# A two-layer hybrid decoder trunk: layer 0's first norm made with tokens on the partitions, and the input loaded twice

## The chip, the core and the metric

The kernel runs on one core of one Trainium2 chip. The metric is device time in microseconds (us) of one launch. The core's engines are TensorE (PE, with its weight loads as PEld), VectorE (DVE), ScalarE (ACT), GpSimd (POOL) and SyncE (SP), which issues all the DMAs spoken of here. Each engine runs its instructions in a fixed order and waits for the others by semaphores.

## What is computed

A sequence of 1024 tokens of width 1024 gets 16 learned tokens in front of it and goes through two layers. Cut to what matters here, the reference is:

```python
def rmsnorm(x, w):
    y = x * lax.rsqrt(jnp.mean(x * x, axis=-1, keepdims=True) + EPS)
    return y * w

h = jnp.concatenate([meta_b, x], axis=1)
for layer in range(DEPTH):
    hn = rmsnorm(h, norm_mix_w[layer])
    proj = hn @ w_in[layer]
    hq, hf, hi, hg, gq, gk, gv, gz, ga, gb, su = jnp.split(proj, pts, axis=-1)
    y_a = hgrn2_mixer(hq, hf, hi, hg, ...)
    y_b = gdn_mixer(gq, gk, gv, gz, ga, gb, ...)
    y_c = s5_mixer(su, ...)
    h = h + jnp.concatenate([y_a, y_b, y_c], axis=-1) @ w_out[layer]
    hn = rmsnorm(h, norm_mlp_w[layer])
    h = h + jnp.square(jax.nn.relu(hn @ mlp_w1[layer])) @ mlp_w2[layer]
return rmsnorm(h, final_norm_w)[:, N_META:]
```

The change is about the very first `rmsnorm` (layer 0, before `w_in`), and about where the `h` of `h + ...` in layer 0 comes from. All is in float32.

## The kernel before

The 1040 tokens are two blocks of 520 tokens; a block is five windows of 104. The 1024 features are eight tiles of 128 partitions, so `h` of a block is eight tiles 128 x 520, with features on the partitions and tokens along the free dimension.

A float32 product is made of three passes on TensorE: each operand is split into a high part rounded to a shorter format and the low part that is left, and the kernel sums high x high, high x low and low x high. `columns` (line 488) does so for 128 output columns: 8 feature tiles x 3 passes x 2 runs of some 260 tokens, 48 matmuls into one PSUM tile `pd`, of which there are two buffers. A weight granule is loaded as `wr` and split into `wh` and `wl` (line 460 and a subtraction). The activation operands are `xh` and `xl` (eight tiles each, 520 tokens and 4 tokens of history in front). Tiles that other stages use under the names `mt`, `qt` and `D2` can serve as a second set of operands; the method that hands them out is `spare_operands`. Scratch tiles `s` have six buffers, and the loads of `x` land in them.

Layer 0 begins like this. `load_x` (line 1276) loads the windows of a block with tokens on the partitions (two DMAs of 104 x 512 a window, line 1288, one more where the 16 learned tokens stand), transposes them on TensorE (line 1291, eight transposes a window) and copies each piece from PSUM to `h`, in turn on ScalarE and VectorE (line 1294): 40 transposes and 40 copies a block. `normed_rows` (line 511) then makes the norm over the features: eight squares, seven additions, a product with a matrix of ones that sums over the partitions (lines 121 to 125), Ln and Exp, and for each of the eight tiles a multiplication by gain and scale (line 116, VectorE, 128 x 520), a cast to the high part (line 532, ScalarE) and a subtraction for the low part (line 113, VectorE). `projection` (line 730) makes all products with `w_in`: first `in_s5` (two output tiles, 96 matmuls, evicted at line 683), then the others, with the decay and solve parts of the DeltaNet between them. In layer 0, block 0, it takes a hook that loads block 1's `x` and saves it. `save_h` stores `h` to DRAM (eight DMAs of 260 KB a block), `states` (the recurrences) follows the projection, and then the same is done for block 1. `run` (line 1466) then reads block 0's `h` back with `get_h`, runs `out_mlp` on it (product with `w_out`, the MLP), makes the norm of layer 1 in the spare operands, saves `h`, and reads block 1's `h` back; that block's `out_mlp` is interleaved with layer 1's projection of block 0.

What stands when on an engine is not written out by hand. A scheduler orders the instructions of each engine at build time by priorities and by its own simulation of the time; on the chip each engine then keeps to that order. DMAs of SP go out in order, over a ring of eight semaphores, so that a DMA waits for the one eight before it.

Of the kernel before, what the change touches and what calls it, by code (L numbers as in the profile page):

```python
# [17 lines left out]
D = 1024  # L18
# [67 lines left out]
def trace(*gens):  # L86

    live = list(gens)
    while live:
        for g in list(live):  # L90
            if next(g, StopIteration) is StopIteration:
                live.remove(g)


class Kern:
# [392 lines left out]
    def columns(self, wts, xs, runs):  # L488

        xh, xl = xs  # L490
        ps = self.tl(self.pd, [128, 2, 512], "pd", 2)
        kn = len(xh)
        for k in range(kn):
            wh, wl = wts[k // 4]
            for i, (w, x) in enumerate(((wh, xh), (wh, xl), (wl, xh))):
                for c, cs in runs.items():
                    self.mm(ps[:, c, :cs.stop - cs.start], w[:, k % 4, :], x[k][:, cs],
                            start=(k == 0 and i == 0), stop=(k == kn - 1 and i == 2))
        return ps
# [10 lines left out]
    def normed_rows(self, h, wcol, b, spare=None):  # L510
# [10 lines left out]
        for k in range(KD):  # L521
# [13 lines left out]
            xs[1].append(lo)  # L535
        return xs

    def normed(self, h, wcol):
# [182 lines left out]

    def block(self, l, b, h, hook=None, first=False):

        xs = self.normed_rows(h, 8 * l, b)
        if first:
            self.save_h(b, h)
        trace(self.projection(l, b, xs, hook, first))
        self.states(l, b)

    def projection(self, l, b, xs, hook=None, first=False):  # L730
# [4 lines left out]
        if first:  # L735
            self.setup_mixers()
        g = {"z": self.tl(self.dr, [6, 128, T], "gated", 2)}
        us = self.in_s5(l, xs)
        yield 2 * DENSE
        g["rows"] = self.in_rows(l, b, xs)  # L740
# [534 lines left out]

    def load_x(self, b, h):
        nc = self.nc
        x = self.ins["x"][0]
        for w in range(NW):
            t0 = b * T + w * W - NMETA  # L1280
            for k0 in (0, 4):
                xt = self.s()[:W, :512]
                cs = slice(128 * k0, 128 * k0 + 512)
                if t0 < 0:
                    nc.sync.dma_start(xt[0:NMETA, :], self.ins["meta"][:, cs])
                    nc.sync.dma_start(xt[NMETA:W, :], x[0:W - NMETA, cs])
                else:
                    nc.sync.dma_start(xt, x[t0:t0 + W, cs])
# [6 lines left out]
            yield  # L1295

# [169 lines left out]
    def run(self):  # L1466
        self.setup()
        self.H, self.YS = {}, {}
        nxt = {}

        def early():

            nxt[1] = self.htiles()
            yield from self.load_x(1, nxt[1])
            self.save_h(1, nxt[1])
# [11 lines left out]

        h = self.get_h(1)
        rest = self.out_mlp(0, 1, h)
# [46 lines left out]
```

## Time and profile before

| | |
|---|---|
| Runs of the kernel | 2992.46 us median of 3 (2989.41 to 2992.55) |
| Profiled execution, own time | 2987.76 us |
| Its span in the trace | 2986.0 us |
| Mean granted TensorE clock | 0.966 of full speed |
| TensorE busy | 2815.6 us (94%) |
| VectorE busy | 1702.9 us (57%) |
| ScalarE busy | 1309.7 us (44%) |
| GpSimd busy | 820.5 us (27%) |

A share of the span is an average over many stages. What a change in one stage is worth is read from that stage. In the rows further down, a timeline row has the start, the duration, the engine, the line and operation with its output and inputs, and in brackets how long the engine sat idle before it and what ended that wait. A row of a stretch has each engine's busy time, then the granted TensorE clock as a share of full speed, then the share of the DMA engines and GB/s. PE durations are modelled and overlap; the distance between two starts is the better measure of a matmul.

### The profile page before, as it was taken

To read this page: it belongs to the slowest core of one execution; us is meant where nothing else is said; L and a number is where in the kernel's file an instruction comes from. 1 tells how busy PE (TensorE), PEld (TensorE's weight loads), DVE (VectorE), ACT (ScalarE), POOL (GpSimd) and SP (SyncE) were. 2 spreads that over 40 slices of the span, in tenths; PEclk is the share of its full clock that TensorE was granted. 3 is DMA by queue.
4 is the path that set the end of the run, shared out by engine and by line. 5 is a ranking of instruction groups with operands and counts; after the bars stand their busy time and mean duration, and the time that the engine had idled before them with its cause. 6 is when DMAs were issued, how large, how long until landed. Compare 5 with 4: busy or idle time off the path is not lost.

```text
span 2986.0 us, 60325 instructions
## 1 busy us (share of the span) xinstructions
PE 2815.6 (94%) x23513; PEld 2632.9 (88%) x23513; DVE 1702.9 (57%) x3497; ACT 1309.7 (44%) x2689; POOL 820.5 (27%) x801
## 2 busy tenths in 40 slices
PE   7797899979999989999999999999899999999998
PEld 6787799878999989998999988987688788999998
DVE  7788885776532245668755577658645323622224
ACT  4455475534443344543434446554344433533332
POOL 0000522154634430000020211101636444144441
PEclk8798999989999999999999999999999999999999
DMA  5666555644433344444633356564544333533332
GB/s 147 185 152 181 161 153 152 185 87 133 123 93 102 92 142 115 123 130 104 167 110 104 116 153 168 155 173 131 129 111 126 90 105 97 162 93 93 93 93 79
DMA packets 641610, 381.17 MB, mean 128 GB/s; under 512 B 166239, under 2 KB 599237, under 8 KB 641325
## 3 DMA queue, kind: packets, MB, share of 16 engines
q1 hardware_dynamic: 641325, 377.31, 45.9%
q8 instruction: 186, 3.05, 0.4%
q14 instruction: 99, 0.81, 0.1%
HBM read 308.52 MB, written 70.43 MB: 127 GB/s over the span
## 4 chain that ended last, share of the span: by engine, by line
PE 78%; DVE 10%; DMA 7%; issue 2%; ACT 1%; POOL 1%; SPq 0%; DVEq 0%; ACTq 0%; POOLq 0%
PE pd L125 66%; PE mxt L125 8%; DVE mh L113 3%; PE mxh L125 3%; DVE wl L113 1%; DVE s L116 1%; DVE s L113 1%; DMA nh<-rowd 1%; DMA XD<-diag 1%; DMA ys<-ydr 1%; DVE mt L113 1%; DMA mh<-qkvd 0%; DMA mh<-rowd 0%; DVE h L113 0%; POOL mh L113 0%
## 5 line engine op out<-in xcount | busy, mean ns | idle before, releaser
L460 ACT CAST wh<-wr 128x512 fp32r<-128x512 f32 x776 | 479.7, 619 | 955.3 <-PE pd L125 879.7
L125 PE MATMUL pd<-xh,wh 128*128 128x260 f32 (+3 forms) x3256 | 737.6, 299 | 25.9 <-DVE s L116 9.0
L125 PE MATMUL pd<-xl,wh 128*128 128x260 f32 (+3 forms) x3256 | 736.9, 299 | 3.7 <-DVE xl L113 2.3
L125 PE MATMUL pd<-xh,wl 128*128 128x260 f32 (+2 forms) x3208 | 719.4, 297 | 2.7 <-POOL wl L113 1.7
L113 POOL TENSOR_TENSOR wl<-wr,wh 128x512 fp32r<-128x512 f32 x376 | 494.2, 1315 | 720.6 <-ACT wh L460 663.1
L125 PEld LDWEIGHTS pd<-xh,wh 128*128 128x128 f32 x3256 | 520.9, 191 | 46.6 <-ACT xh L532 7.5
L125 PEld LDWEIGHTS pd<-xl,wh 128*128 128x128 f32 x3256 | 522.1, 191 | 19.9 <-DVE xl L113 3.0
L125 PEld LDWEIGHTS pd<-xh,wl 128*128 128x128 f32 x3208 | 514.6, 191 | 17.0 <-POOL wl L113 2.3
L125 PE MATMUL pd<-uh,wh 128*128 128x260 f32 (+1 forms) x2008 | 469.3, 303 | 14.1 <-DVE h L113 8.0
L125 PE MATMUL pd<-uh,wl 128*128 128x260 f32 (+1 forms) x2008 | 472.1, 303 | 0.0
L125 PE MATMUL pd<-ul,wh 128*128 128x260 f32 (+1 forms) x2008 | 468.0, 302 | 0.7 <-DVE ul L113 0.6
L113 DVE TENSOR_TENSOR h<-h,pd 128x520 f32<-128x520 f32 (+2 forms) x296 | 200.4, 678 | 347.6 <-PE pd L125 345.3
L125 PEld LDWEIGHTS pd<-uh,wh 128*128 128x128 f32 x2008 | 321.0, 189 | 30.1 <-issue 6.8
L113 DVE TENSOR_TENSOR wl<-wr,wh 128x512 fp32r<-128x512 f32 x400 | 282.0, 705 | 106.2 <-ACT wh L460 101.6
L125 PEld LDWEIGHTS pd<-uh,wl 128*128 128x128 f32 x2008 | 322.5, 189 | 14.2
L125 PEld LDWEIGHTS pd<-ul,wh 128*128 128x128 f32 x2008 | 321.1, 189 | 14.2 <-DVE ul L113 1.3
L110 ACT ACTIVATE s<-s 128x520 f32<-128x520 f32 (+3 forms) x431 | 272.6, 636 | 120.6 <-DVE s L121 55.1
L116 DVE SCALAR_TENSOR_TENSOR s<-pd,r 128x520 f32<-128x520 f32 (+2 forms) x121 | 83.6, 692 | 249.8 <-PE pd L125 249.7
L113 DVE TENSOR_TENSOR s<-s 128x520 f32<-128x520 f32 (+3 forms) x199 | 137.8, 696 | 54.9 <-ACT s L110 53.4
L113 DVE TENSOR_TENSOR ul<-s,uh 128x520 fp32r<-128x520 f32 (+1 forms) x129 | 93.8, 729 | 114.6 <-ACT uh L460 114.0
L113 POOL TENSOR_TENSOR nt<-nt 128x208 f32<-128x208 f32 x80 | 54.2, 678 | 367.1 <-ACT nt L110 247.7
L403 POOL MEMSET mh<- 128x512 f32 x2 | 1.1, 526 | 496.0 <-DVE RT L113 294.6
(272 smaller groups left out, 3549.8 us busy)
## 6 DMA issues: line engine op xcount, KB each, us to landing
wr<-in_mlp_w_dram SPq DMA_DIRECT2D x512, 256.0 KB
wr<-in_w_in_dram SPq DMA_DIRECT2D x208, 256.0 KB
wr<-in_w_out_dram SPq DMA_DIRECT2D x64, 256.0 KB
qkvd<-s SPq DMA_DIRECT2D x48, 260.0 KB
win<-qkvd SPq DMA_DIRECT2D x40, 312.0 KB
hdr<-h SPq DMA_DIRECT2D x32, 260.0 KB
mh<-qkvd SPq DMA_DIRECT2D x40, 208.0 KB
hd<-s SPq DMA_DIRECT2D x32, 260.0 KB
```

Source lines behind the costliest of these rows:

```text
L110: return self.nc.scalar.activation(out, in_, func, **kw)
L113: return (eng or self.nc.vector).tensor_tensor(out, a, b, op)
L116: return self.nc.vector.scalar_tensor_tensor(out, a, s, b, op0, op1)
L125: return self.nc.tensor.matmul(out, lhsT, rhs, start=start, stop=stop, **kw)
L403: nc.gpsimd.memset(z, 0.0)
L460: self.nc.scalar.copy(hi, src)
```

## The change

Layer 0's norm is no longer made from `h`. A new `load_normed` loads a window of `x` with tokens on the partitions, and there sums the squares of each token (two ScalarE Squares with an accumulator, one addition), takes Ln and Exp on 104 x 1, scales the window's two halves in place (two VectorE operations 104 x 512), and transposes the scaled rows into one `pd` tile. From there each of the eight pieces 128 x 104 goes straight into the operands: ScalarE writes the high part with the gain as its scale, VectorE the low part (gain times piece, less the high part). So a window has eight pairs of one ScalarE and one VectorE operation, a block 40. Block 0 uses the spare operands, block 1 `xh` and `xl`, in the hook within block 0's projection. The norm's other setup is moved ahead of the loads. In layer 0's first projection `in_s5` goes over the first run of tokens alone, and then over the second. The stores of `h` and the reloads before `out_mlp` go away for layer 0. In their place `load_x` loads `x` again before each block's `out_mlp`, with 40 transposes and 40 copies each.

```diff
-        for k in range(kn):
-            wh, wl = wts[k // 4]
-            for i, (w, x) in enumerate(((wh, xh), (wh, xl), (wl, xh))):
-                for c, cs in runs.items():
...
+        for part in [{c: cs} for c, cs in runs.items()] if self.early else [runs]:
+            for k in range(kn):
+                wh, wl = wts[k // 4]
+                for i, (w, x) in enumerate(((wh, xh), (wh, xl), (wl, xh))):
+                    for c, cs in part.items():
...
+    def load_normed(self, b, spare=None):
...
+        nxt = self.x_rows(b, 0)
+        yield
+        for w in range(NW):
+            rows, nxt = nxt, self.x_rows(b, w + 1) if w + 1 < NW else None
+            ss = self.tl(self.sp, [W, 4], "xss", 2)
+            for i, xt in enumerate(rows):
+                junk = self.s()[:W, :512]
+                self.act(junk, xt, AF.Square, accum_out=ss[:, i:i + 1])
+            self.tt(ss[:, 2:3], ss[:, 0:1], ss[:, 1:2], ALU.add)
+            self.act(ss[:, 2:3], ss[:, 2:3], AF.Ln, scale=1.0 / D, bias=EPS)
+            self.act(ss[:, 3:4], ss[:, 2:3], AF.Exp, scale=-0.5)
+            ps = self.tl(self.pd, [128, 2, 512], "pd", 2)
+            for g, xt in enumerate(rows):
+                self.ts(xt, xt, ss[:, 3:4], ALU.mult)
+                for i in range(4):
+                    nc.tensor.transpose(ps[:, g, i * W:(i + 1) * W], xt[:, i * 128:(i + 1) * 128], self.ident[:W, :W])
+            at = slice(HIST + w * W, HIST + (w + 1) * W)
+            for k in range(KD):
+                p, wc = ps[:, k // 4, (k % 4) * W:(k % 4 + 1) * W], self.prm[:, k:k + 1]
+                self.act(xs[0][k][:, at], p, AF.Copy, scale=wc)
+                self.stt(xs[1][k][:, at], p, wc, xs[0][k][:, at].bitcast(F32), ALU.mult, ALU.subtract)
+            yield
...
-        h = self.htiles()
-        trace(self.load_x(0, h))
+        self.first, self.early = None, False
+        load = self.load_normed(0, self.spare_operands())
+        next(load)
+        self.setup_norms()
+        trace(load)
         self.ready = {(0, col): self.in_weights(0, col) for col in (C_SU, C_SU + 128)}
-        self.setup_norms()
-        self.block(0, 0, h, early(), True)
-        self.block(0, 1, nxt[1])
-        h = self.get_h(0)
+        xs = self.first
+        trace(self.projection(0, 0, xs, self.load_normed(1), True))
+        xs = self.first
+        self.states(0, 0)
+        trace(self.projection(0, 1, xs))
+        self.states(0, 1)
+        h = self.load_x(0)
         trace(self.out_mlp(0, 0, h))
         self.low = None
         xs = self.normed_rows(h, 8, 0, self.spare_operands())
         self.save_h(0, h)
 
-        h = self.get_h(1)
+        h = self.load_x(1)
         rest = self.out_mlp(0, 1, h)
```

The order of instructions changes at three places that matter below.

TensorE at the start, before; `pd_202` is the last piece of the last window, `pd_275` the sum of squares, and `pd_478` and `pd_532` the two products of `in_s5`:

```order
L1291 MATMUL pd_191<-ident_88,s_189 128x104 x4
L220 MATMUL mxh_247<-ident_88,mh_237 128x128
L1291 MATMUL pd_202<-ident_88,s_200 128x104 x4
L230 MATMUL mxh_364<-ident_88,mh_362 128x96
L125 MATMUL pd_275<-s_251,ones_235 128x260 x2
L125 MATMUL pd_478<-xh_285,wh_214 128x264
L125 MATMUL pd_478<-xh_285,wh_214 128x256
L125 MATMUL pd_532<-xh_285,wh_226 128x264
```

and after the change; lines 566 and 331 are the window's transposes and those of the S5 parameters, `mt_91` is the first high part:

```order
L566 MATMUL pd_221<-ident_88,s_172 128x104 x4
L566 MATMUL pd_260<-ident_88,s_209 128x104 x4
L566 MATMUL pd_260<-ident_88,s_211 128x104 x4
L331 MATMUL mxh_464<-ident_88,mh_402 128x16
L331 MATMUL mxh_464<-ident_88,mh_403 128x16
L331 MATMUL mxh_464<-ident_88,mh_402 128x16
L566 MATMUL pd_295<-ident_88,s_248 128x104 x4
L566 MATMUL pd_295<-ident_88,s_250 128x104 x4
L331 MATMUL mxh_464<-ident_88,mh_403 128x16 x2
L125 MATMUL pd_479<-mt_91,wh_341 128x264
L125 MATMUL pd_479<-mt_92,wh_341 128x264
```

All five windows' transposes and those of the S5 parameters now stand ahead of the first product, and `pd_479` takes the buffer of `pd_260`, the fourth window's.

TensorE at the change from block 0 to block 1 of layer 0, after the change; `pd_3590` is the last product of block 0's projection and `xh_1876` block 1's first operand:

```order
L125 MATMUL pd_3590<-mt_99,wh_3587 128x260 x2
L125 MATMUL pd_3590<-mt_100,wh_3587 128x260 x2
...
L125 MATMUL pd_3590<-D2_106,wh_3587 128x260 x2
L125 MATMUL pd_3590<-D2_105,wl_3586 128x260 x2
L125 MATMUL pd_5067<-xh_1876,wh_5058 128x264
L125 MATMUL pd_5067<-xh_1876,wh_5058 128x256
```

Before, the sum of squares `pd_4983` and the norm's casts stood between the two; now the products follow each other.

TensorE at the second load of block 1 after the change; `pd_14062` is the last product of block 0's MLP, `pd_14112` the sum of squares of layer 1's norm, `pd_14330` layer 1's first product:

```order
L125 MATMUL pd_14062<-uh_13827,wl_14058 128x260 x2
L125 MATMUL pd_14112<-s_14088,ones_115 128x260 x2
L1338 MATMUL pd_14210<-ident_88,s_14206 128x104 x4
L1338 MATMUL pd_14219<-ident_88,s_14208 128x104 x4
...
L1338 MATMUL pd_14298<-ident_88,s_14294 128x104 x4
L1338 MATMUL pd_14307<-ident_88,s_14296 128x104 x4
L125 MATMUL pd_14330<-mt_14122,wh_14321 128x264
L125 MATMUL pd_14330<-mt_14122,wh_14321 128x256
```

Before, layer 1's first product stood right behind the sum of squares; now ten groups of four transposes stand between them, each group in a `pd` buffer of its own.

## Rows read from the trace of the kernel before

**Rows 1.** The page: engines over the span, and the chain that ended last.
```profile
PE 2815.6 (94%) x23513; PEld 2632.9 (88%) x23513; DVE 1702.9 (57%) x3497; ACT 1309.7 (44%) x2689; POOL 820.5 (27%) x801
...
PE 78%; DVE 10%; DMA 7%; issue 2%; ACT 1%; POOL 1%; SPq 0%; DVEq 0%; ACTq 0%; POOLq 0%
```

**Rows 2.** Stretches of the change of block and what follows (start:end, length, engines, PEclk).
```profile
248.80:273.90 25.10, 9.68 (x34) 7.44 (x35) 22.09 (x43) 13.91 (x30) 0.39 (x1) 0.59 0.36 112
...
300.00:330.00 30.00, 22.13 (x241) 20.14 (x241) 28.42 (x64) 12.77 (x26) 19.55 (x21) 0.77 0.47 129
```

**Rows 3.** Timeline of PE at the change of block in layer 0.
```profile
248.40 0.40 PE L125 MATMUL pd<-xh,wl 128*128 128x260 f32 x2
...
266.40 1.24 PE L125 MATMUL pd<-xh,wh 128*128 128x264 f32 x4 [2.50 <-ACT xh L532]
...
273.52 0.54 PE L125 MATMUL pd<-xh,wl 128*128 128x264 f32 x2
273.90 0.40 PE L125 MATMUL pd<-xh,wh 128*128 128x264 f32 x2
```

**Rows 4.** One tile's instructions (ns min/median/max), and a group of the page (busy, mean).
```profile
L116 DVE SCALAR_TENSOR_TENSOR s<-h,prm,r x16: 741/748/755, 30.7 to 275.1; 128x520 f32<-128x520 f32 x16
```
```profile
L113 DVE TENSOR_TENSOR s<-s 128x520 f32<-128x520 f32 (+3 forms) x199 | 137.8, 696 | 54.9 <-ACT s L110 53.4
```

**Rows 5.** Timeline of ACT and DVE at the first window.
```profile
7.72 0.24 ACT L1294 COPY h<-pd 128x104 f32<-128x104 f32 x1 [1.42 <-PE pd L1291]
8.00 0.27 DVE L1294 COPY h<-pd 128x104 f32<-128x104 f32 x1 [0.97 <-ACT h L1294]
8.30 0.24 ACT L1294 COPY h<-pd 128x104 f32<-128x104 f32 x1 [0.33 <-DVE h L1294]
```

**Rows 6.** Forms near the new ones, from four tiles' instructions (ns min/median/max).
```profile
L1294 ACT COPY h<-pd x40: 218/245/253, 7.7 to 142.3; 128x104 f32<-128x104 f32 x40
L1294 DVE COPY h<-pd x40: 247/266/268, 8.0 to 143.5; 128x104 f32<-128x104 f32 x40
L110 ACT ACTIVATE xh<-h,prm x8: 713/728/733, 574.8 to 617.7; 128x520 fp32r<-128x520 f32 x8
L532 ACT CAST xh<-s x8: 623/623/627, 31.6 to 40.7; 128x524 fp32r<-128x524 f32 x8
L116 DVE SCALAR_TENSOR_TENSOR nt<-mxt,gsc,mt x20: 334/343/352, 341.3 to 547.0; 104x128 f32<-104x128 f32 x20
```

**Rows 7.** Timeline of DVE and PE at the start.
```profile
19.10 0.22 DVE L222 COPY prm<-mxh 128x56 f32<-128x56 f32 x1 [0.51 <-PE mxh L220]
...
32.27 1.24 PE L125 MATMUL pd<-xh,wh 128*128 128x264 f32 x4 [3.86 <-ACT xh L532]
...
49.77 0.65 DVE L683 COPY s<-pd 128x264 f32<-128x264 f32 x1
```

**Rows 8.** Timeline of PE around the hook's load of block 1.
```profile
109.28 0.41 PE L125 MATMUL pd<-xh,wl 128*128 128x264 f32 x2
...
123.89 1.62 PE L1291 MATMUL pd<-ident,s 104*128 104x104 f32 x8 [8.88 <-DMA s<-in_x_dram]
...
142.84 0.51 PE L125 MATMUL pd<-xh,wh 128*128 128x264 f32 x2 [0.65 <-DVE h L1294]
```

**Rows 9.** PE around the first product of `out_mlp`, block 0, and that stretch's engines.
```profile
540.38 0.41 PE L125 MATMUL pd<-xh,wl 128*128 128x260 f32 x2
...
560.37 0.80 PE L125 MATMUL pd<-uh,wh 128*128 128x260 f32 x4 [0.18 <-ACT uh L460]
```
```profile
540.80:560.40 19.60, 14.47 (x84) 12.40 (x83) 9.71 (x25) 10.37 (x38) 5.90 (x7) 0.66 0.75 209
```

**Rows 10.** Timeline of PE and ACT at layer 1's first products.
```profile
1115.87 1.23 PE L125 MATMUL pd<-mt,wh 128*128 128x264 f32 x4 [5.01 <-ACT mt L532]
...
1119.08 0.80 PE L125 MATMUL pd<-mt,wh 128*128 128x264 f32 x2 [1.98 <-DVE mt L113]
...
1123.57 0.63 ACT L532 CAST D<-s 128x524 fp32r<-128x524 f32 x1
```

More of the change, by code (lines that the diff above doesn't have):

```diff
@@ L536, in normed_rows @@
         return xs
+    def load_normed(self, b, spare=None):
+        nc = self.nc
+        before, self.first = self.first, ([], [])
+        for k in range(KD):
+            for half_, tag in zip(self.first, ("xh", "xl")):
+                half_.append(next(spare) if spare else self.operand(tag))
+        xs = self.first
+        if before is None:
+            zero = self.sp.tile([128, HIST], F32, name="zero")
+            nc.vector.memset(zero, 0.0)
+        nxt = self.x_rows(b, 0)
[15 more added lines that the diff above has]
+            at = slice(HIST + w * W, HIST + (w + 1) * W)
+            for k in range(KD):
+                p, wc = ps[:, k // 4, (k % 4) * W:(k % 4 + 1) * W], self.prm[:, k:k + 1]
+                self.act(xs[0][k][:, at], p, AF.Copy, scale=wc)
+                self.stt(xs[1][k][:, at], p, wc, xs[0][k][:, at].bitcast(F32), ALU.mult, ALU.subtract)
+            yield
+        for i in range(2):
+            for k in range(KD):
+                nc.scalar.copy(xs[i][k][:, :HIST], before[i][k][:, T:].bitcast(F32) if before else zero)
     def normed(self, h, wcol):
@@ L720, in lead, with block @@
             yield
[L722 to L727, printed above, removed]
+    def block(self, l, b, h):
+        trace(self.projection(l, b, self.normed_rows(h, 8 * l, b)))
         self.states(l, b)
@@ L737, in projection @@
         g = {"z": self.tl(self.dr, [6, 128, T], "gated", 2)}
+        self.early = first
         us = self.in_s5(l, xs)
+        self.early = False
         yield 2 * DENSE
@@ L1274, in htiles, with x_rows, load_x @@
         return [self.tl(self.big, [128, T], "h", 8) for _ in range(KD)]
-    def load_x(self, b, h):
+    def x_rows(self, b, w):
         nc = self.nc
         x = self.ins["x"][0]
-        for w in range(NW):
[L1280 to L1288, printed above, removed]
+        t0 = b * T + w * W - NMETA
+        rows = []
+        for k0 in (0, 4):
+            xt = self.s()[:W, :512]
+            cs = slice(128 * k0, 128 * k0 + 512)
+            if t0 < 0:
+                nc.sync.dma_start(xt[0:NMETA, :], self.ins["meta"][:, cs])
+                nc.sync.dma_start(xt[NMETA:W, :], x[0:W - NMETA, cs])
+            else:
+                nc.sync.dma_start(xt, x[t0:t0 + W, cs])
+            rows.append(xt)
+        return rows
+    def load_x(self, b):
+        nc = self.nc
+        h = self.htiles()
+        for w in range(NW):
+            for k0, xt in zip((0, 4), self.x_rows(b, w)):
                 ps = self.tl(self.pd, [128, 2, 512], "pd", 2)[:, 0, :]
@@ L1294, in load_x @@
                     copy(h[k0 + i][:, w * W:(w + 1) * W], ps[:, i * W:(i + 1) * W])
-            yield
+        return h
     def save_h(self, b, h):
@@ L1468, in run @@
         self.H, self.YS = {}, {}
[L1469 to L1475, printed above, removed]
-        h = self.htiles()
-        trace(self.load_x(0, h))
-        self.ready = {(0, col): self.in_weights(0, col) for col in (C_SU, C_SU + 128)}
-        self.setup_norms()
-        self.block(0, 0, h, early(), True)
-        self.block(0, 1, nxt[1])
-        h = self.get_h(0)
+        self.first, self.early = None, False
[3 more added lines that the diff above has]
+        trace(load)
+        self.ready = {(0, col): self.in_weights(0, col) for col in (C_SU, C_SU + 128)}
+        xs = self.first
+        trace(self.projection(0, 0, xs, self.load_normed(1), True))
+        xs = self.first
+        self.states(0, 0)
+        trace(self.projection(0, 1, xs))
+        self.states(0, 1)
+        h = self.load_x(0)
         trace(self.out_mlp(0, 0, h))
```

4 lines of the change are left out of this document (2 added, 2 removed).

## The prediction

> **What bounds the kernel.** I read the page first: TensorE is busy in 94% of the span, and 78% of the chain that ended last is its own [rows 1]. So what counts is where TensorE stands idle or runs at the lower clock, and the change can only move such places; its own 80 added transposes are small beside them. I then read the five places that the change touches, one by one, in the timeline of TensorE and in rows of a stretch, and the durations of single forms. The reader should see in them how long TensorE goes without a product, and who is late there.
>
> **The change of block, the gain.** Before, the last product of block 0 starts at 248.40, the first of block 1 at 266.40, and products follow each other at the lower clock until 273.90, where their distance falls from 0.43 to 0.24 us [rows 3]. The stretch of 25.1 us holds some 21 products (4 at 266.40 and some 17 up to 273.90), at 0.12 each 2.5 us, and I allow 2 us for the ones-products and S5 transposes: 20.6 us are lost. In the new order the products of block 1 follow at once, for its operands are made in the hook. But VectorE was busy in 22.09 of those 25.1 us [rows 2], and part of that is not the norm: the norm's share is 8 x 0.748 for the gain and 15 x 0.696 for seven additions and eight low parts (the last form lies nearest), together 16.4 us [rows 4]. What is late next is VectorE with the S5 and DeltaNet work of that stage, which moves up by the 16.4 us and by what TensorE's waiting had cost it, 25.1 - 22.09 = 3.0. So the gain lies between 16.4 and 19.4; I take **18**, with 13 if some of the 3.0 and the norm's cover turns out to be waits for DMA, and 22 if it reaches the 20.6 and a little of the next stretch. Up to 28 is a rival below: from 300 to 330 TensorE is busy 22.13 of 30 us at clock 0.77, with VectorE at 28.42 [rows 2].
>
> **The price of a pair.** In the old load the copies of a piece take turns: ScalarE at 7.72, VectorE at 8.00, ScalarE again at 8.30, the latter after 0.33 of waiting for VectorE though they write different tiles [rows 5]. So a pair of copies takes 0.58 us, and a block has 20 pairs. The new load has 40 pairs of a high and a low part, and the order of ScalarE shows the same wait on VectorE ahead of each high part. The high part with a scale is not in the trace at this size; a scaled one of 520 columns takes 0.728 against 0.623 for a plain cast, so I add 0.105 to the 0.245 of the copy; the low part I take at 0.343 (104 x 128 from PSUM) instead of 0.266 [rows 6]. A pair then takes 0.58 + 0.105 + 0.077 = 0.76. Its bounds are 0.58 (no dearer than copies) and, if the turns overlap between two windows, about 0.45 (VectorE's 0.343 and one small operation).
>
> Row and rule together: the row at 8.30 shows the wait, but not whether the chip needs it. The Trainium skill's page "PSUM — Partial Sum Buffer", section "PSUM bank collisions raise a hardware error", says that two engines, reads of ScalarE and VectorE included, must not be in one bank and quadrant at once and that hardware does not arbitrate. By it the pairs of a window could not overlap under any order, and 40 of them would cost the 30 us of the serial price; without it the estimate would be VectorE's time alone, some 14. No run here shows a collision.
>
> **The start.** The norm's squares, additions and wide passes go away, the pairs come. A pair needs the gains `prm`, which are copied at 19.10 before [rows 7] and stand ahead of the first transposes now; I set the first pair at 13, about midway between 7.7 (the first copy [rows 5]) and 19. `pd_479` needs the fourth window's buffer, so 32 pairs must be done: 13 + 32 x 0.76 = 37.3, and with some 60 small S5 operations between the pairs on VectorE I take 40. From there 96 products take some 14 us without waits, to 54. Before, the first product is at 32.27, comes in pieces behind the casts, and the second product's eviction starts at 49.77 [rows 7]. That is 4 later: **+4**. Bounds: 0 (pairs at 0.58: 13 + 18.6 = 31.6, with the small operations 36) and +9 (first pair at 19).
>
> **The hook.** Before, TensorE has its last product at 109.28, goes to block 1's transposes at 123.89 after a wait for the DMA of `x`, and products go on at 142.84 [rows 8]. 40 pairs take 30.4 us against 11.6 for the copies, 18.8 more. Part is covered: the 8.88 us wait for `x` and VectorE's gaps hide the early windows, but the last two windows' 16 pairs come after their loads, 16 x 0.76 - 8 x 0.58 = 7.5 dearer, and queued behind them on both engines is the decay work that TensorE waits for next. Some idle time of the following 30 us is taken up. I take **+5**, bounds 0 and +9. The eight stores of `h` that left are DMAs that nobody waits for: nothing, and if the queue was what held back `x`, a gain of a microsecond or two that the bound 0 holds.
>
> **The second load of block 0.** Before, TensorE goes from the last projection product at 540.38 to the first of `out_mlp` at 560.37, busy with the recurrences' tail in 14.47 of 19.6 us at clock 0.66; VectorE is busy for 9.71, ScalarE for 10.37 [rows 9]. In the new order ten groups of four transposes stand among that tail, each with four copies in turns: 2 x 0.58 = 1.16 us a group, 11.6 in all. The two engines are half idle there, so about half hides: **+5**. Bounds: -1 (the reload of `h` by DMA is not late any more) and +11 (nothing hides).
>
> **The second load of block 1.** Here nothing hides. Before, layer 1's first products stand at 1115.87 and go on from 1119.08 as operands come, the last operand's cast starting at 1123.57 [rows 10]. In the new order all ten groups of transposes stand in front of the first product, and their copies on ScalarE and VectorE behind seven of the eight casts. So: copies from about 1123, 10 x 1.16 = 11.6, first product near 1134.5, at the lower clock at first. The products before 1123.9 (4.8 us at half speed from 1119.08 and four at 1115.87) would take 2.9 at full clock, so before counts as a start at 1121.0; 1134.5 - 1121.0 is 13.5, and 1.5 for the lower clock makes **+15**. Bounds: +11 (copies at once, no clock lost) and +18 (1.4 a group).
>
> **Sum.** 4 + 5 - 18 + 5 + 15 = **+11** on the profiled execution's 2987.76: 2998.8. The median of the runs lies 4.7 above that execution, so I forecast **3003**. Later the order of layer 1's instructions differs here and there; I price that at nothing, with 4 either way. The split `in_s5` adds no instruction and lies in the start's term.
>
> **Rivals.** A measurement of this kernel can tell 0.2% from no change, that is 6 us: under 2986.5 is faster, over 2998.4 slower.
>
> - *The forecast* (chance 0.55): slower, 2996 to 3011.
> - *VectorE's gain runs on* (0.20): the stretch from 300 to 330 is VectorE's (28.42 of 30), and 7.9 us of TensorE's idle time and clock 0.77 stand there. If the 16.4 us of removed work also close those, the change of block gives 28, and the sum is +1: 2993. It decides if TensorE is busy over 9.5 of 10 us in what is now 300 to 330. Against it: the later tail needs loads that do not move up.
> - *Pairs overlap* (0.17), the case on the other side: in the new order the pairs of two windows alternate, so one window's high part can run during the other's low part. At 0.45 a pair the start gives 13 + 14.4 and with the rest -4, the hook 0, the second load of block 0 hides wholly (0), that of block 1 gives +11: -4 + 0 - 18 + 0 + 11 = -11, 2981. It decides below some 0.5 us a pair.
> - *The loads starve* (0.08): before, TensorE waited 8.88 us for `x` in the hook [rows 8] behind busy scratch buffers and queue. If both second loads wait as well, they cost +11 and +22, the hook +9: with +4 and -18 the sum is +28, 3020.
>
> That the change does not do what it says I leave out: the order shows the moved norm, the pairs and the transposes.
>
> **Numbers.** The likeliest case gives 3003. The range from 2985 to 3016 holds the forecast, the case at 2993 and the near edges of the outer two; left out are most of their 0.17 and 0.08. Some of the forecast's lower edge lies under 2998.4: same 0.22, slower 0.60, and 0.18 for faster.
>
> **What would show it.** Right: block 1's products behind block 0's within 1 us at what was 248.8; high parts at 0.35 us and pairs near 0.76; layer 1's first product some 13 later, relative to the ones-products, than before; ten groups of transposes at 1.2 to 1.4 us each. Wrong: pairs at 0.5 or less; layer 1's first products not behind the copies but a few microseconds after the casts; the change of block giving 25 or more; or the first product before 35.

## The result and the profile after

The changed kernel takes 3010.35 us (median of 6 runs) against 2991.76 for the kernel before, measured beside it: a ratio of 1.0078, with a 95% interval from 1.0063 to 1.0094. The interval excludes 1, so it is slower. The two medians lie 18.6 us apart; the ratio on record stands for some 23 us. The profiled execution has a span of 3009.3 us against 2986.0 before, 23.3 more, so the trace can tell where the time went, within the few us by which single executions differ.

The page of the changed kernel answers to [rows 1]:

```profile
PE 2825.3 (94%) x23585; PEld 2641.1 (88%) x23585; DVE 1712.4 (57%) x3562; ACT 1331.6 (44%) x2809; POOL 823.8 (27%) x793
```

Nothing of the 23 us shows there. TensorE's busy time grows by 10 us, and the shares stay. So I follow the same instructions through both traces. Each row of this table is one eviction of a product by VectorE, taken by its count among its like; its start before, its start after, and the lag:

```
                                                     before    after     lag
second product of in_s5 (block 0)                      49.8     57.4    +7.6
last convolution product ahead of the hook            109.7    118.9    +9.2
first convolution product behind the hook             153.3    187.9   +34.6
tenth gate product, near the end of block 0           249.3    286.7   +37.4
first product of block 1                              281.6    296.1   +14.6
last gate product of layer 0                          540.8    553.0   +12.2
first product of out_mlp, block 0                     573.9    590.1   +16.2
last product of block 0's MLP                        1106.8   1121.4   +14.7
first product of layer 1                             1128.3   1157.7   +29.4
end of the span                                      2986.0   3009.3   +23.3
```

The stages read off it as differences of lags: the start +9.2, the hook +28.2 (37.4 - 9.2), the change of block -22.8 (and -2.4 more until 540.8), the second load of block 0 +4.0, that of block 1 +14.7 (29.4 - 14.7), and -6.1 in layer 1's later order with -1.5 in block 0's MLP. The sum is +23.3. The hook's +28.2 rests on these rows, two before and the same two after:

```profile
109.71 0.76 DVE L116 SCALAR_TENSOR_TENSOR s<-pd,cvw,s 128x520 f32<-128x520 f32 x1
249.30 0.69 DVE L121 TENSOR_SCALAR s<-pd 128x520 f32<-128x520 f32 x1
```
```profile
118.91 0.75 DVE L116 SCALAR_TENSOR_TENSOR s<-pd,cvw,s 128x520 f32<-128x520 f32 x1
286.70 0.69 DVE L121 TENSOR_SCALAR s<-pd 128x520 f32<-128x520 f32 x1
```

Between the rows of the table the lag is not flat: in block 1's projection it is +25.4 at one eviction and +6.2 at a later one. So a stage's term depends by some us on the row it is read at.

**The start and the hook.** The timeline of TensorE in the changed kernel, first at the start, then in the hook:

```profile
43.56 0.81 PE L125 MATMUL pd<-mt,wh 128*128 128x264 f32 x2 [0.85 <-DVE D L116]
...
136.09 1.65 PE L566 MATMUL pd<-ident,s 104*128 104x104 f32 x8 [12.37 <-DVE s L121]
141.77 3.07 PE L125 MATMUL mxt<-mh 128*104 128x104 f32 x16 [4.04 <-DMA mh<-qkvd]
150.96 1.69 PE L125 MATMUL mxt<-mh 128*104 128x104 f32 x8 [3.56 <-DMA mh<-qkvd]
154.32 1.69 PE L125 MATMUL mxt<-mh 128*104 128x104 f32 x8 [1.68 <-DMA mh<-qkvd]
163.97 1.65 PE L566 MATMUL pd<-ident,s 104*128 104x104 f32 x8 [6.57 <-DVE xl L116]
167.66 1.65 PE L566 MATMUL pd<-ident,s 104*128 104x104 f32 x8 [2.04 <-DVE xl L116]
173.71 1.25 PE L125 MATMUL pd<-mt,wh 128*128 128x264 f32 x4 [4.41 <-DVE xl L116]
```

The first product comes at 43.56, against 32.27 [rows 7]. In the hook the transposes run from 136.09 to 169, 33 us, where the old ones took from 123.89 to about 141 [rows 8], and products go on at 173.71. From the first transposes to the next product that is 37.6 us, against 19.0 before. TensorE waits in turn for a window's scaling, for the decay work's reloads, and for low parts. The pairs themselves, from the tiles' instructions in the hook and a piece of the timeline:

```profile
L110 ACT ACTIVATE xh<-pd,prm x40: 324/347/348, 137.8 to 176.6; 128x104 fp32r<-128x104 f32 x40
L116 DVE SCALAR_TENSOR_TENSOR xl<-pd,prm,xh x40: 301/318/327, 138.2 to 177.3; 128x104 fp32r<-128x104 f32 x40
```
```profile
L121 DVE TENSOR_SCALAR s<-s,xss x20: 465/478/487, 12.8 to 163.2; 104x512 f32<-104x512 f32 x20
```
```profile
164.68 0.35 ACT L110 ACTIVATE xh<-pd,prm 128x104 fp32r<-128x104 f32 x1 [1.41 <-DVE xl L116]
165.06 0.33 DVE L116 SCALAR_TENSOR_TENSOR xl<-pd,prm,xh 128x104 fp32r<-128x104 f32 x1 [0.41 <-ACT xh L110]
165.42 0.58 ACT L110 ACTIVATE xh<-pd,prm 128x104 fp32r<-128x104 f32 x2 [0.39 <-DVE xl L116]
```

A pair in turns takes 165.42 - 164.68 = 0.74 us; from 165.42 on, with the pieces of two windows at hand, two pairs take that time, 0.37 us each. The 40 of the hook spread over 39 us, since decay steps and solve stand between them. Their VectorE work is 40 x 0.318 and 10 x 0.478, 17.5 us, where the old copies in the hook had 20 x 0.266 = 5.3, so 12.2 us more.

**The change of block.** TensorE at the change of block, in the changed kernel:

```profile
285.38 0.40 PE L125 MATMUL pd<-D,wl 128*128 128x260 f32 x2
285.62 0.40 PE L125 MATMUL pd<-xh,wh 128*128 128x264 f32 x2
```

The engines in the hook (120 to 180) and behind it (160 to 200), before:

```profile
120.00:180.00 60.00, 48.10 (x353) 45.86 (x354) 42.00 (x115) 27.69 (x72) 0.00 (x0) 0.83 0.67 186
160.00:200.00 40.00, 38.62 (x317) 38.05 (x315) 37.95 (x78) 19.61 (x33) 0.00 (x0) 1.00 0.55 148
```

and after, with the stretch behind the change of block:

```profile
120.00:180.00 60.00, 23.74 (x132) 21.73 (x133) 44.78 (x145) 32.39 (x123) 0.00 (x0) 0.57 0.45 113
160.00:200.00 40.00, 21.43 (x130) 19.98 (x131) 36.17 (x101) 13.22 (x41) 0.00 (x0) 0.67 0.16 37
285.00:310.00 25.00, 24.79 (x304) 23.05 (x302) 21.87 (x47) 12.55 (x27) 17.64 (x22) 1.00 0.81 233
```

Block 1's products follow at 0.24 us, at full clock, where [rows 2, 3] had 25 us with the clock at 0.59. But in the 40 us from 160 TensorE is busy in 21.43, where it had 38.62 before: the hole has moved ahead. VectorE was already busy in 37.95 of these 40 us before the change, so work that is pushed into this stretch finds little room. In the hook itself, from 120 to 180, VectorE is busy in 44.78 of 60 us, 2.8 more than before and not full; there TensorE waits for the chain of the windows, as the rows above show.

**The second loads.** TensorE at layer 1's first products, answering to [rows 10], and the issue of the loads:

```profile
1124.07 2.07 PE L125 MATMUL pd<-s,ones 128*128 128x260 f32 x4 [3.03 <-DVE s L113]
1138.23 1.74 PE L1338 MATMUL pd<-ident,s 104*128 104x104 f32 x8 [12.09 <-DMA s<-in_x_dram]
...
1147.53 1.96 PE L1338 MATMUL pd<-ident,s 104*128 104x104 f32 x8 [0.21 <-DVE h L1341]
1149.70 1.23 PE L125 MATMUL pd<-mt,wh 128*128 128x264 f32 x4 [0.21 <-DVE h L1341]
```
```profile
1135.26 7.82 SPq L1327 DMA_DIRECT2D s<-in_x_dram  x10
```
```profile
1137.27 0.62 ACT L534 CAST qt<-s 128x524 fp32r<-128x524 f32 x1
1139.19 0.24 ACT L1341 COPY h<-pd 128x104 f32<-128x104 f32 x1 [1.30 <-PE pd L1338]
```

The ten groups take from 1138.23 to 1149.70, 1.15 us each. Ahead of them TensorE waits 12.09 us for `x`, whose loads are issued at 1135.26. By the order of the code they land in the scratch tiles that the norm of layer 1 fills, and the subtractions that free these run on VectorE from 1133.31. But the wait is not all a price of the late `x`: in ScalarE's order the first copy stands behind the seventh cast, which ends at 1137.89, and ScalarE then waits only 1.30 us for the first transposes.

### The profile page after: what moved, and what is told of

It is laid out like the page before. It is cut to its first block, busy times and chain, and to the rows that moved or that the text cites. A ratio compares the mean times of both kernels' runs of the same rounds, so it can differ in the third digit from the quotient of the medians.

```text
span 3009.3 us, 60581 instructions
## 1 busy us (share of the span) xinstructions
PE 2825.3 (94%) x23585; PEld 2641.1 (88%) x23585; DVE 1712.4 (57%) x3562; ACT 1331.6 (44%) x2809; POOL 823.8 (27%) x793
## 5 line engine op out<-in xcount | busy, mean ns | idle before, releaser
L125 PE MATMUL pd<-xh,wh 128*128 128x260 f32 (+4 forms) x2824 | 647.0, 300 | 12.7 <-DVE h L113 6.3
L125 PE MATMUL pd<-xl,wh 128*128 128x260 f32 (+4 forms) x2824 | 641.9, 299 | 1.3 <-DVE xl L116 1.3
L125 PE MATMUL pd<-xh,wl 128*128 128x260 f32 (+2 forms) x2792 | 634.1, 298 | 0.9 <-POOL wl L113 0.9
L125 PEld LDWEIGHTS pd<-xh,wh 128*128 128x128 f32 (+1 forms) x2824 | 451.0, 189 | 31.1 <-DVE h L113 6.7
L125 PEld LDWEIGHTS pd<-xl,wh 128*128 128x128 f32 (+1 forms) x2824 | 451.5, 190 | 15.5 <-DVE xl L116 1.5
L125 PEld LDWEIGHTS pd<-xh,wl 128*128 128x128 f32 x2792 | 447.8, 190 | 14.6 <-POOL wl L113 1.2
L110 ACT ACTIVATE s<-s 128x520 f32<-128x520 f32 (+4 forms) x451 | 284.4, 635 | 108.5 <-DVE s L121 46.6
L125 PE MATMUL pd<-mt,wh 128*128 128x264 f32 (+3 forms) x1188 | 207.3, 293 | 14.9 <-DVE s L116 7.3
L125 PEld LDWEIGHTS pd<-mt,wh 128*128 128x128 f32 (+1 forms) x1188 | 174.0, 195 | 17.6 <-issue 6.7
L113 DVE TENSOR_TENSOR s<-s 128x520 f32<-128x520 f32 (+3 forms) x185 | 130.0, 706 | 58.1 <-ACT s L110 56.2
```

Of the source, the lines that this page charges most:

```text
L110: return self.nc.scalar.activation(out, in_, func, **kw)
L113: return (eng or self.nc.vector).tensor_tensor(out, a, b, op)
L125: return self.nc.tensor.matmul(out, lhsT, rhs, start=start, stop=stop, **kw)
```

## Experiments

In the jobs of these runs the kernel before took 2981 to 2985 us in the median, so I compare ratios to it, and the lags of the table above at single places.

**1. Block 1's normed load behind block 0's projection.**

```diff
-        trace(self.projection(0, 0, xs, self.load_normed(1), True))
+        trace(self.projection(0, 0, xs, None, True))
+        trace(self.load_normed(1))
```

> The changed kernel, but block 1's normed load is written behind the whole projection of block 0 and not in the middle of it. Theory 'place' (the hook costs some 30 us because the windows' loads, transposes and pairs are chained window by window among the decay steps, with their DMA reloads, while no product can run): the products between 110 and 240 us lose the 30 us, and part of it, 5 to 15, comes back where block 1 begins; 2985 to 3000 us. Rival 'price' (40 pairs in turns are 30 us of ScalarE and VectorE wherever they stand): the same 30 us are lost at the change of block instead, 3005 to 3015.

Measured: 1.0125 (1.0108 to 1.0142), slower than the changed kernel and over both expectations. The lag at the first convolution behind the hook's old place goes from +34.6 to -22.0: measured from the lag ahead of the hook, without any load there the products come 29.9 us earlier than in the kernel before, so the old load costs 30 us there, and the new form 55 (25.4 + 29.9). From the tenth gate product (-13.4) to the first product of block 1 (+7.1), 20.5 us are lost, where the changed kernel gains 22.8. TensorE waits there as it did in the hook:

```profile
242.59 1.65 PE L566 MATMUL pd<-ident,s 104*128 104x104 f32 x8 [8.84 <-DVE s L121]
257.51 1.65 PE L566 MATMUL pd<-ident,s 104*128 104x104 f32 x8 [9.38 <-DVE xl L116]
```

So most of the load's price comes along to the new place, but not all: at the last gate product of layer 0 the lag is +5.5, against +12.2 in the changed kernel. That this run is the slower one comes only later: some 8 us are lost in block 0's MLP, in a later order that I did not follow.

**2. The hook cut into windows, one behind each dense product.**

```diff
-        if hook:
-            trace(hook)
         for i in range(8, 12):
             self.in_conv(l, b, xs, i)
+            if hook:
+                next(hook, None)
...
             self.in_gate(l, xs, C_GZ + 128 * i, g["z"][i])
+            if hook:
+                next(hook, None)
```

> The changed kernel with block 1's normed load cut into its five windows, one behind each of the next dense products of block 0's projection. Theory 'place': each window hides behind 48 matmuls, the hook's 30 us go, 2980 to 2990 us. Rival 'price': a window's eight pairs take 6 us and hold one of the two PSUM tiles, so each product beside it waits about as long; at most 10 us return, 3000 to 3010.

Measured: 1.0158 (1.0143 to 1.0173), worse than either expectation. The waits of TensorE from 108 to 262 us begin with:

```profile
PE pd L566 <- DVE s L121: 33.6, 4, 12.9
PE mxt L125 <- DMA mh<-qkvd: 8.7, 1, 8.7
```

Four windows each keep TensorE waiting for their scaled rows, 33.6 us in all: in its fixed order a window's transposes stand between products while the window is not ready. Spreading does not hide them.

**3. The old norm, with the second loads.** The kernel before without `save_h` and `get_h` in layer 0:

```diff
-        h = self.get_h(0)
+        h = self.htiles()
+        trace(self.load_x(0, h))
...
-        h = self.get_h(1)
+        h = self.htiles()
+        trace(self.load_x(1, h))
```

> The kernel before, with the norm as it was, but without the stores and reloads of layer 0's residual; x is loaded and transposed again before the two output stages, as in the changed kernel. Theory (the second loads cost 4 and 14 us on the path): 3005 to 3013 us against 2992. Rival (they are hidden, and what the changed kernel shows there comes from its other order): 2990 to 2997.

Measured: 1.0069 (1.0051 to 1.0087), as the theory said, at its upper edge. The lag steps by 7.8 us at the first load (-4.0 to +3.8) and by 14.1 at the second (-1.7 to +12.4). So without the new norm the first load costs 4 us more than in the changed kernel, and the second as much. At the second, the same two parts appear: a wait for `x`, and then ten groups.

```profile
1121.96 1.62 PE L1289 MATMUL pd<-ident,s 104*128 104x104 f32 x8 [13.18 <-DMA s<-in_x_dram]
...
1133.43 1.23 PE L125 MATMUL pd<-mt,wh 128*128 128x264 f32 x4 [0.46 <-DVE h L1292]
```

**4. The second load of block 1 cut into windows behind layer 1's first steps.** `again` is the load as a generator.

```diff
         for n in self.projection(1, 0, xs):
             due += n
+            if next(again, StopIteration) is not StopIteration:
+                continue
```

> The changed kernel with the second load of block 1 cut into its five windows, one behind each of the first five steps of layer 1's projection, and the output stage's steps begun after that. Theory (the load costs 14 us because all ten groups of transposes and their copies stand in front of the first product): 2994 to 3000 us. Rival (the groups share the two PSUM tiles with the products, so the copies cost as much there): 3006 to 3012.

Measured: 1.0223 (1.0206 to 1.0239), against both. Layer 1's first product has its lag back (+13.8, a step of 1.1 instead of 14.7), but between 1140 and 1220 TensorE stops at each window:

```profile
PE pd L1342 <- DMA s<-in_x_dram: 26.2, 6, 5.4
```

Six waits for `x` make 26.2 us. A window's loads stand in SP's order behind weight loads of the projection, and go out right behind them, for example:

```profile
1194.15 3.34 SPq L482 DMA_DIRECT2D wr<-in_w_out_dram  x2
1197.58 0.85 SPq L1327 DMA_DIRECT2D s<-in_x_dram  x2
```

The transposes of that window start at 1200.97, behind 5.01 us of waiting. And the output stage's products, which would fill such gaps, come later by this edit. How much each of the two costs was not separated.

**5 and 6. Other PSUM for the pieces, first try: the one bank of the small products.**

```diff
-            ps = self.tl(self.pd, [128, 2, 512], "pd", 2)
+            pp = [self.mps("h"), self.mps("h")]
```

(experiment 5, for block 1's normed load; experiment 6 does the like in `load_x`.)

> The changed kernel, in which block 1's normed load puts its transposed pieces into the single PSUM bank of the small products (half a window at a time) and not into the two tiles of the dense products. Theory 'tile' (in the hook no product can run because windows whose pairs wait hold both product tiles, so the products stand still for all five windows): products go on among the windows, 20 to 30 us of the hook's 31 come back, 12 to 22 us less than the changed kernel in all. Rival 'turns' (the pairs in turns and the decay work on VectorE and ScalarE set the pace, whichever PSUM they use): within 6 us of the changed kernel.

> The changed kernel, in which the two second loads put their transposed pieces into the single PSUM bank of the small products. Theory 'tile' (the 4 and 16 us come from pieces that hold both product tiles ahead of the first product): layer 1's first product follows the casts, 14 to 20 us less than the changed kernel. Rival 'turns' (the copies on ScalarE and VectorE take as long and the products wait for them in TensorE's order): within 6 us of the changed kernel, or slower with one bank in place of two tiles.

Measured: 1.0272 (1.0251 to 1.0294) and 1.0451 (1.043 to 1.0471). Experiment 5 misses both expectations. Experiment 6 misses its theory; its rival allowed for 'slower with one bank in place of two tiles' without a figure. The loss has a reason of its own. TensorE's waits in experiment 5 from 110 to 330 us:

```profile
PE mxh L418 <- DVE nh L121: 28.6, 2, 23.9
PE mxh L434 <- DVE mh L113: 27.6, 4, 23.0
```

Buffers of one kind are handed round in the order of the code. In experiment 5 the one bank is shared by solve, S5 parameters and windows, and they wait for each other. In experiment 6 most of the loss stands at the load of block 0: the lag at the first product of `out_mlp` is +252.7. These two runs decide nothing on the question.

**7. The second load of block 1 in the recurrences' three banks.**

```diff
-                ps = self.tl(self.pd, [128, 2, 512], "pd", 2)[:, 0, :]
+                ps = self.mps("t") if b else self.tl(self.pd, [128, 2, 512], "pd", 2)[:, 0, :]
```

> The changed kernel, in which only the second load of block 1 leaves the two tiles of the dense products: its pieces go into the three PSUM banks that the recurrences use, which are free there. Theory 'tile' (layer 1's first product waits for copies because all ten groups stand in product tiles ahead of it): the 16 us come back, 2992 to 2998 us, 12 to 18 less than the changed kernel. Rival 'turns' (the copies take ScalarE and VectorE from the casts and splits that the products need): less than 6 us come back.

Measured: 1.0044 (1.0032 to 1.0056), some 10 us under the changed kernel's 1.0078. That lies between the two expectations (12 to 18 back, or less than 6), nearer to the theory. The step at layer 1's first product falls from 14.7 to 4.2 (+8.1 to +12.3). The products now stand ahead of the transposes:

```profile
1117.55 2.07 PE L125 MATMUL pd<-s,ones 128*128 128x260 f32 x4 [3.03 <-DVE s L113]
1125.29 1.24 PE L125 MATMUL pd<-mt,wh 128*128 128x264 f32 x4 [5.67 <-ACT mt L534]
1128.50 0.80 PE L125 MATMUL pd<-mt,wh 128*128 128x264 f32 x2 [1.98 <-DVE mt L113]
1134.59 1.23 PE L1338 MATMUL mxt<-ident,s 104*128 104x104 f32 x12
```

So most of what the load of block 1 costs comes from its pieces sitting in the product tiles ahead of the first product.

**8. The same banks for the hook's normed load.** The edit of experiment 5 with `self.mps("t")`.

> The changed kernel, in which block 1's normed load in the hook uses those three banks. Theory 'tile' (products stand still in the hook because waiting windows hold both product tiles): 15 to 30 us less than the changed kernel. Rival 'turns' (the pairs, their scratch and the decay work set the pace): within 8 us of the changed kernel.

Measured: 1.0102 (1.0081 to 1.0123), 7 us over the changed kernel, with intervals that overlap: within the rival's bound, and far from the theory. The lag at the tenth gate product still grows by 23.7 in the hook (8.0 to 31.7). The tiles do hold up the first products: at the first convolution behind the hook the lag is +19.3, where the changed kernel has +34.6. But of these 15 us only 6 are left at the tenth gate product, and in between VectorE is full:

```profile
180.00:200.00 20.00, 15.04 (x93) 14.27 (x93) 20.00 (x42) 6.12 (x15) 0.00 (x0) 0.75 0.16 44
```

So the product tiles are not what decides the hook's loss. That it is the pairs' turns, as the rival says, this run does not show; the next one speaks against it.

**9. The old norm at the new place.** The kernel before, with block 0's norm in the spare operands and block 1's made in the hook:

```diff
             yield from self.load_x(1, nxt[1])
             self.save_h(1, nxt[1])
+            nxt["xs"] = self.normed_rows(nxt[1], 0, 1)
...
-        self.block(0, 0, h, early(), True)
-        self.block(0, 1, nxt[1])
+        xs = self.normed_rows(h, 0, 0, self.spare_operands())
+        self.save_h(0, h)
+        trace(self.projection(0, 0, xs, early(), True))
+        self.states(0, 0)
+        trace(self.projection(0, 1, nxt["xs"]))
+        self.states(0, 1)
```

> The kernel before, with its own loads, copies, stores and reloads, in which only the place of two norms' operands changes: block 0's norm goes into the spare operands, and block 1's norm is made in the hook, behind its load. Theory (the gain at the change of block comes from the move, the loss in the hook from the form with pairs): the change of block gains 20 to 30 us, the hook loses 5 to 12 for the norm's 16 us of VectorE, 2970 to 2982 us against 2992, faster than both kernels. Rival (a norm in the hook costs 30 us in whichever form): 2990 to 3000.

Measured: 1.0013 (1.0003 to 1.0023): within the rival's range, though the hook costs 24 us and not 30. The lag is -0.4 ahead of the hook, +23.6 at the tenth gate product, -3.1 at block 1's first, and +8.8 at the last gate product of layer 0. So the move alone, with the old form, costs 24 us in the hook and gives 27 back at the change of block, of which 12 are lost again by the end of layer 0 (the changed kernel keeps them). The two kernels do not lose at the same place: at the first convolution behind the hook the lag has grown by 14 here and by 25 in the changed kernel. The stretch from 160 to 200:

```profile
160.00:180.00 20.00, 16.07 (x109) 15.89 (x108) 19.65 (x46) 9.66 (x18) 0.00 (x0) 0.83 0.56 163
180.00:200.00 20.00, 12.52 (x102) 12.06 (x100) 19.79 (x32) 5.93 (x10) 0.00 (x0) 0.87 0.46 118
```

VectorE is busy in 39.4 of 40 us, GpSimd in none.

Together with experiment 3 this accounts for the result: the second loads alone give +0.69%, the move of the norm alone +0.13%, and the changed kernel has +0.78%. The changed kernel's later start (+9.2) and its later order (-7.6) are in neither, so the agreement rests in part on these two cancelling.

**10. The same, with the eight subtractions on GpSimd.**

```diff
-            self.tt(lo, xn, hi.bitcast(F32), ALU.subtract)
+            self.tt(lo, xn, hi.bitcast(F32), ALU.subtract, eng=self.nc.gpsimd if b and wcol == 0 else None)
```

> The last kernel (the norm of block 1 in the hook, in its old form), with the eight subtractions of that norm's low parts on GpSimd, which is idle there, and not on VectorE. Theory 'VectorE' (the hook's 23 us are VectorE's: from 160 to 200 us it is busy 19.7 of 20, so that work which moves there only moves the loss): 5.6 us of VectorE's work go, 4 to 8 us come back in the hook, and the whole lies at 2974 to 2981 us where the kernel before has 2983, faster than it. Rival 'chain' (the hook's loss is the chain from load to last operand, for which a slower subtraction is no help): no change or up to 5 us slower than without it.

Measured: 0.9996 (0.9984 to 1.0008). That is 5 us less than experiment 9, as the theory said of the hook, but level with the kernel before and not faster, as it said of the whole. The lag at the tenth gate product falls from +23.6 to +17.5, and the same stretch reads:

```profile
160.00:180.00 20.00, 16.27 (x129) 15.69 (x128) 19.90 (x35) 9.72 (x20) 13.95 (x8) 1.00 0.56 163
180.00:200.00 20.00, 16.86 (x135) 16.06 (x133) 19.93 (x37) 9.51 (x17) 0.00 (x0) 1.00 0.47 125
```

VectorE is as full, TensorE has 4.5 us more of busy time at full clock. Some 5.5 us of VectorE's work gave 6 us there: in this kernel VectorE bounds this stretch.

**11. Experiment 7, with the Squares' unused output in another kind of scratch.**

```diff
-                junk = self.s()[:W, :512]
+                junk = self.big6()[:W, :512]
```

> The changed kernel with the second load of block 1 in the recurrences' PSUM banks (as above), in which the Squares of the normed loads write their unused output into a scratch tile of another kind and not into the six that the windows of x are loaded into. Theory 'scratch' (loads and Squares wait for scratch tiles that transposes free late, 5 us in the hook): 5 to 12 us less than that kernel, from the start and the hook. Rival 'turns and VectorE' (pairs in turns and VectorE's other work set the pace): within 4 us of it.

Measured: 1.0035 (1.0024 to 1.0046), 3 us under experiment 7, within the rival's bound. The lag at the tenth gate product is +35.9, not less than experiment 7's +34.1. The scratch that the Squares use does not set the hook's pace.

**12. Experiment 10, with the hook's copies all on ScalarE.**

```diff
-                    copy = nc.vector.tensor_copy if i % 2 else nc.scalar.copy
+                    copy = nc.vector.tensor_copy if i % 2 and b == 0 else nc.scalar.copy
```

> The kernel with the old norm of block 1 in the hook and its subtractions on GpSimd, in which the hook's 40 copies of transposed pieces all run on ScalarE and none on VectorE. Theory 'VectorE' (what leaves VectorE in the hook comes back in time): 20 x 0.27 = 5.3 us of VectorE's work go and the turns with them, 3 to 8 us less than the kernel without this, so 2970 to 2978 us where the kernel before has about 2982, and faster than it. Rival 'chain' (the copies come before VectorE is full, and the load from DRAM and ScalarE's 40 copies in a row set their pace): within 3 us of the kernel without this.

Measured: 1.0019 (1.0009 to 1.0029), 7 us over experiment 10: against the theory, and outside the rival's 3 us too. The transposes still follow the loads of `x`, for example:

```profile
125.31 1.62 PE L1291 MATMUL pd<-ident,s 104*128 104x104 f32 x8 [9.05 <-DMA s<-in_x_dram]
```

The copies come before VectorE is full (in experiment 10 it is busy in 9.00 of 20 us from 120 to 140), and VectorE time that leaves there brought nothing. From 160 to 200 TensorE is busy in 28.02 us, against 33.12 in experiment 10. Why this run came out slower and not level I did not find.

## Why the prediction was right, and where it was wrong

The direction was right and so was the range, but the total of +11 was put together from terms of which one was far off. That 3010 still lies in the range is in part luck: two other terms, the change of block and the later order, came out 15 us better than forecast, and without them the hook's miss of 23 us would have carried it beyond 3016.

- *The change of block* (forecast -18): -22.8, and about -25 with what follows until 540.8. Right in kind. The forecast's own sign of being wrong, 25 or more, stands at this edge, but the sign of the rival in which the gain runs on did not come: in what was 300 to 330, TensorE is busy in 27.22 of 30 us and not over 9.5 of 10.

```profile
320.00:350.00 30.00, 27.22 (x349) 24.99 (x348) 25.47 (x59) 14.79 (x38) 10.64 (x13) 0.97 0.69 199
```

- *The hook* (forecast +5, bounds 0 to +9): **+28.2**. This is the step that failed. I charged the hook only with the 18.8 us that 40 pairs take more than 20 pairs of copies, and let the wait for `x`, gaps of VectorE and later idle time cover all but 5. Nothing was covered: from the first transposes to the next product the hook takes 18.7 us more than before (37.6 against 19.0), the first transposes come 3.0 us later against the lag ahead of the hook, behind Squares and scalings that I had not priced, and 6.5 more are lost by the tenth gate product. Part of the reason is that the norm's work of VectorE had not gone away. I credited 16.4 us of it to the change of block, and of these 12.2 come back in the hook in the new form; and the stretch behind the hook, whose idle time was to take up some of it, had VectorE busy in 37.95 of 40 us already before the change. Experiment 9 shows that the place costs this much and not only the form: with the old form there, 24 us are lost. Experiment 10 shows that in that kernel the stretch behind the hook is VectorE's; for the changed kernel this is argued from its rows and from experiment 8, not tested by a run that takes VectorE's work away.
- *The price of a pair* (0.76): 0.74 in turns. The turns also overlap between two windows, as the rival had it, down to 0.37 a pair from 165.42 on, which is under the 0.5 named as a sign of being wrong. That rival's times did not follow: TensorE waits for the chain of a window from load to low part, not for pairs that stand side by side.
- *The start* (forecast +4, bounds 0 to +9): +9.2, at the upper bound. The first product came at 43.56 and not at 40, mainly because the first high part started at 17.19 and not at 13.

```profile
17.19 0.33 ACT L110 ACTIVATE mt<-pd,prm 128x104 fp32r<-128x104 f32 x1
```

- *The second load of block 0* (forecast +5): +4.0 here and +7.8 in experiment 3.
- *The second load of block 1* (forecast +15): +14.7 here and +14.1 in experiment 3. Right in size and in mechanism. The ten groups took 11.5 us ahead of the first product, and their copies stood behind seven of the eight casts, as forecast. TensorE's 12.09 us of waiting for `x` looks like the rival 'the loads starve', but the seventh cast ends only 1.3 us before the first copy, so by these rows the late `x` adds about that much. Experiment 7 shows that the groups cost little once they stand behind the products.
- *Later order* (forecast 0, 4 either way): -7.6, with MLP and layer 1 together, outside its bound. Not followed, and the cause stays open.

The sum of the misses: +23 in the hook, +5 at the start, -1 and 0 at the loads, -7 at the change of block, -8 later, 12 in all, which is 23 against the forecast 11.

Weighed against the Trainium skill's page "PSUM — Partial Sum Buffer", section "PSUM bank collisions raise a hardware error": the pairs of a window kept their turns here, and those of two windows, in different tiles, did overlap. No run here took the turns away, so whether the chip needs them was not tried. The prediction drew too much from the section when it said that the pairs of a window could not overlap under any order: the rule is stated by bank and quadrant, and a window's tile has two halves of 512 floats, each as large as the single bank of experiment 5.

What stays open: which part of the 24 us in the hook of experiment 9 is VectorE's 16.4 us of moved work and which is the waits that it starts (experiment 10 took back 6 for 5.5), how much of the changed kernel's 28 us is VectorE's and how much the chain of its windows, and why experiment 12 is slower. No version found is faster than the kernel before; experiment 10 is level with it.

## What to carry to other kernels

When a step is moved, book its whole work where it goes, on the engine that is full there, and not only what its new form adds: a hole in TensorE's time that closes in one place can open in another of the same size. Before moving it, read the busy share of the engine that does the work in the stretch that receives it; here that row, 37.95 of 40 us, was in the trace of the kernel before. A load that is repeated late should not stand in the tiles of the products that follow it; experiment 7 took 10 of 15 us off by that alone. Landing tiles of its own for the late load were not tried.

## Not expected of the hardware

Each Square with an accumulator is followed on ScalarE by an instruction of its own that reads the sum:

```profile
133.34 0.63 ACT L110 ACTIVATE s<-s 104x512 f32<-104x512 f32 x1 [1.95 <-DMA s<-in_x_dram]
133.88 0.19 ACT L110 ACTIVATION_READ_ACCUMULATOR s<-s 104x1 f32 x1
```

And the subtraction on GpSimd in experiment 10 took 1.776 us in the median and up to 4.207 with VectorE full beside it:

```profile
L113 POOL TENSOR_TENSOR xl<-s,xh x8: 1281/1776/4207, 158.3 to 172.3; 128x524 fp32r<-128x524 f32 x8
```
